# A state-space and expert block on one core: expert weights in pairs of units, more gathered rows per unit, six splits moved to GpSimd, two loads moved ahead

## The chip, the core and the metric

One core of a Trainium2 chip. The time is device microseconds from launch to end; it is the median of several runs, and lower is better. A profile is one execution recorded by the hardware profiler; its span runs from the first to the last instruction.

## What is computed

One layer on 512 frames of 1024 channels (with 16 meta frames ahead of them): a state-space mixer and a gated short convolution are merged into the stream `h`; then an expert layer (PEER) adds to it, and a last norm gives the output. The change touches only the expert layer:

```python
q = (xb @ w_q).reshape(PEER_BLOCK, PEER_HEADS, 2, PEER_HALF)
s = jnp.einsum('thjd,hjkd->thjk', q, sub_keys)      # 8 heads x 2 halves x 128 keys
sv, si = lax.top_k(s, 16)                           # then the best 16 of 16 x 16 sums
eidx = i1 * 128 + i2;  g = softmax(cs)              # 128 experts of 16384 per frame
act = gelu(einsum('td,thkd->thk', xb, u[eidx]))
out = einsum('thk,thkd->td', g * act, v[eidx])
```

All is float32; the large products are made from splits of each operand into a rounded part (hi) and a remainder (lo), with three matmuls for one.

## The kernel before, in words

The expert layer has 512 frames: 128 of them (tile 0) take their 128 + 128 expert rows by gather, the other 384 (`TD`) take all 16384 experts densely, in 128 units of 128 experts. Its work stands in four stretches.

1. **Routing** (lines 642 to 687). 16 query tiles; VectorE (DVE) picks the best 16 of every score tile (`top16`, lines 634 to 639, five instructions for each of 64 lists, more later in `choose`).
2. **The first 72 U units** (`S_AHEAD`, lines 902 to 917). For each unit `Stream` (lines 139 to 163) loads a 512 KB tile `raw` on SyncE's (SP's) queue, ScalarE (ACT) rounds it to `whi` (line 155), DVE makes `wlo` (line 156; an argument `lo` may name GpSimd, POOL, for chosen units), and TensorE (PE) does 24 matmuls of 384 columns into `sps`. Three `whi`/`wlo` buffers exist. ACT makes the gelu `so` (line 896), SP stores it to scratch `asc` (line 905). Beside that DVE makes the dense gates, which go to scratch `gsc` (lines 911 and 917).
3. **First V stretch**, n = 0 to 55 of the loop at lines 972 to 986. PE does the remaining 56 U units (three ahead, line 973) and for each n 18 matmuls of 512 columns of V (line 983) into `vps`. The weights of a unit (lines 957 to 966) are `wt` = gelu x gates (DVE, line 963), `wh` (ACT, line 964) and `wl` (DVE, line 965), each 128 x 384, made two units ahead (`WLEAD`); four `wh` and `wl` buffers. Gates come from `gsc` in tiles `gt` for four units (line 939). The V tile of a unit is loaded (line 152) and split (lines 155, 156) one unit ahead.
4. **Second V stretch**, n = 56 to 127: V alone, with the gelu reloaded from `asc` (line 946). The matmuls of the last three units are done together, frame tile by frame tile (`VTAIL`, line 977).

**The gathered rows** (lines 856 to 878) run beside stretches 3 and 4: POOL issues an indirect load of one row tile (line 862, four ahead, six buffers), DVE takes it (line 872 for 128 U rows, then line 874 for 128 V rows). How many are taken per unit is written out by hand: after unit n the program takes rows until 1.15 x `RATE` is used up, a row being 1.15 (`ROW`), with `RATE` 2.7 in stretch 3 and 1.0 in stretch 4. What is left stands behind the loop (line 987). Rows of unit n are queued on DVE behind that unit's V split and behind the last `wl` (line 985).

Then `final` (lines 575 to 602) goes through the four frame tiles: for tiles 1 to 3 the V sums are added (line 587), two squares with a sum on ACT (line 588), small DVE steps (lines 591 to 594, `rsqrt` at 127 to 132), two scalings (599, 601) and two stores (602). Tile 0 needs the last gathered row.

The order of the instructions on each engine is fixed when the program is built: a planner goes by program order, and lets a later instruction pass one that it expects to wait.

Of the kernel before, what the change touches and what calls it, by code (L numbers as in the profile page):

```python
# [11 lines left out]
F32 = mybir.dt.float32  # L12
R = mybir.dt.float32r
# [4 lines left out]
OP = mybir.AluOpType  # L18
# [4 lines left out]
P = 128  # L23
D = 1024
# [12 lines left out]
NK = 128  # L37
# [4 lines left out]
TD = T - P  # L42
# [6 lines left out]
S_FIRST = 5  # L49
HALVED = 3  # L50
PLAG = 2
S_BUFS = 4
ROW = 1.15
BUDGET = 3.1
GY = 0.2
# [1 line left out]
GT = 32  # L57
GL = 4
RLEAD = 4
WLEAD = 2  # L60
VTAIL = 3
RATE = (2.7, 1.0)


def build(nc, tc, ctx, a):
    def pool(name, bufs=1, space=None, stack=None, **kw):
        if space is not None:
            kw["space"] = space
        return (stack or ctx).enter_context(tc.tile_pool(name=name, bufs=bufs, **kw))

    V = nc.vector
    A = nc.scalar
    PL = nc.gpsimd
# [10 lines left out]
    rawp = pool("rawp", bufs=4)  # L84
    hlp = pool("hlp", bufs=3)
# [53 lines left out]
    class Stream:  # L139
# [6 lines left out]
            self.i, self.q, self.ahead = 0, [], ahead  # L146
            self.lo = lo or (lambda i: V)

        def _emit(self):
            i = self.i  # L150
            r = self.rawp.tile([P, D], F32, name="raw", tag="raw")
            self.load = nc.sync.dma_start(r, self.ap[self.order[i]])
            hi = self.hlp.tile([P, D], R, name="whi", tag="whi")
            lo = self.hlp.tile([P, D], R, name="wlo", tag="wlo")
            A.copy(hi, r)  # L155
            self.last = self.lo(i).tensor_tensor(lo, r, hi.bitcast(F32), op=OP.subtract)  # L156
            self.q.append((hi, lo))
            self.i += 1

        def next(self):  # L160
            while self.i < self.n and len(self.q) < 1 + self.ahead:
                self._emit()
            return self.q.pop(0)

    def norm_rows(pl, tiles, rows, ss):
# [30 lines left out]
    with xst:  # L196
# [46 lines left out]
        e = pi.tile([P, 5, H], F32, name="sp_e")  # L243
        z = pi.tile([P, 5, H], F32, name="sp_z")
        z2 = pi.tile([P, 5, H], F32, name="sp_z2")
        q = pi.tile([P, 5, H], F32, name="sp_q")
# [23 lines left out]
        act = pi.tile([H, NT, P], F32, name="act")  # L270
# [171 lines left out]
    def step():  # L442

        for q in scans[:2]:
            q[1] += 1
            if next(q[0], True):
                scans.remove(q)
            if scans and scans[0] is q and q[1] < 7:
                break
# [54 lines left out]
    for d in range(KD):  # L504
        ps_y = psC.tile([P, T], F32, name="ps_y", tag="ps_y")
        for u in range(2):
            hi, lo = wb.next()
# [5 lines left out]
        hi, lo = wb.next()  # L513
# [21 lines left out]
    with ExitStack() as st:  # L535
# [12 lines left out]
        for tp in range(2):  # L548
            pss = [[psC.tile([P, T], F32, name="ps_o", tag=("ps_y", "ps_c")[hf]) for hf in range(2)]
                   for _ in range(2)]  # L550
            for u in range(8):
                hi, lo = wo.next()
# [7 lines left out]
            for ti in range(2):  # L560
                t = 2 * tp + ti
                for hf in range(2):
                    o = slice(hf * 512, (hf + 1) * 512)
# [11 lines left out]
    def final(out, psp, lnf):  # L575
        with ExitStack() as st:
            pf = pool("pf", bufs=2, stack=st)
            nc.sync.dma_start(lnf, a["ln_final"].partition_broadcast(P))
            for t in range(NT):
# [15 lines left out]
                for hf in range(2):  # L595
# [6 lines left out]
                    nc.sync.dma_start(a["out"][t * P:(t + 1) * P, cs_], o)  # L602

    peer(nc, tc, ctx, a, pool, dram, rawp, hlp, ident, Stream, mm3, acc, u2h, u2l, u2d, ft512, psS, final)


def peer(nc, tc, ctx, a, pool, dram, rawp, hlp, ident, Stream, mm3, acc, u2h, u2l, u2d, ft512, psS, final):

    V, A, PL, PE = nc.vector, nc.scalar, nc.gpsimd, nc.tensor
    gsc = dram.tile([TD // GT, P, NK, GT], F32, name="gsc")  # L610
    asc = dram.tile([S_AHEAD, P, TD], F32, name="asc")
# [10 lines left out]
    sdot = pk.tile([P, PH * TOPK], F32, name="sdot")  # L622
    S_out = pool("sout", bufs=S_BUFS, stack=pp)

# [255 lines left out]
    def advance(gen, us):  # L880
        while us > 0:
            c = next(gen, None)
            if c is None:
                return us
            us -= c
        return us

    us = Stream(a["u_t"], rawp, hlp, ahead=2)

    def scores(dst):  # L890
        ps = psS.tile([P, T], F32, name="sps", tag="s")
        hi, lo = us.next()
        for k in range(KD):
            ks = slice(k * P, (k + 1) * P)
            mm = mm3(ps[:, :TD], hi[:, ks], lo[:, ks], u2h[:, k, P:], u2l[:, k, P:], k == 0, k == KD - 1)
        return mm, A.activation(dst, ps[:, :TD], AF.Gelu)  # L896
# [3 lines left out]
    gdebt = 0.0  # L900
    debt = 0.0
    for e in range(S_AHEAD):
        o = S_out.tile([P, TD], F32, name="so", tag="so")
        mm, act = scores(o)
        nc.sync.dma_start(asc[e], o)
        with ExitStack() as after:
            for i in (mm, act, anchor[0]):
                if i is not None:
                    after.enter_context(tc.issue_after(i.ins))
            for _ in range(min(NSTORE, len(stores))):  # L910
                nc.sync.dma_start(*stores.pop(0))
            if e >= S_FIRST:
                debt = advance(gates, BUDGET + debt)
    for _ in gates:
        pass
    while stores:
# [7 lines left out]
    pv = pool("pv", bufs=2, stack=rows, side="right")  # L924
# [4 lines left out]
    order = list(range(S_AHEAD, NK)) + list(range(S_AHEAD))  # L929
    vs = Stream(a["v"].rearrange("(u p) d -> u p d", p=P), rawv, hlv, order=order,  # L930
                lo=lambda i: V)
    out = [psV.tile([P, 2, 512], F32, name=f"vps{t}", tag=f"vps{t}") for t in range(ND)]
    loaded = {}

    def load_gates(n):
        if n % GL == 0:
            e = order[n]
            loaded["gt"] = pv.tile([P, TD // GT, GL, GT], F32, name="gt", tag="gt")
            nc.sync.dma_start(loaded["gt"], gsc[:, :, e:e + GL].rearrange("h p i t -> p h i t"))
        return loaded["gt"][:, :, n % GL]  # L940

    def load_gelu(n):
        if n % 2 == 0:
            e = order[n]
            loaded["al"] = rawp.tile([P, D], F32, name="raw", tag="raw")[:, :2 * TD].rearrange("p (i t) -> p i t", i=2)
            nc.sync.dma_start(loaded["al"], asc[e:e + 2].rearrange("i p t -> p i t"))
        return loaded["al"][:, n % 2]

    direct, wlast = [], [None]

    def ahead(n):
        if n < NK - S_AHEAD:
            o = S_out.tile([P, TD], F32, name="so", tag="so")
            scores(o)
            direct.append(o)

    def weights(n):
        gt = load_gates(n)
        ac = direct.pop(0) if order[n] >= S_AHEAD else load_gelu(n)
        wt = pv.tile([P, TD], F32, name="wt", tag="wt")  # L960
        wh = pv.tile([P, TD], R, name="wh", tag="wh", bufs=4)
        wl = pv.tile([P, TD], R, name="wl", tag="wl", bufs=4)
        V.tensor_tensor(wt.rearrange("p (h t) -> p h t", t=GT), ac.rearrange("p (h t) -> p h t", t=GT), gt, op=OP.mult)
        A.copy(wh, wt)  # L964
        wlast[0] = V.tensor_tensor(wl, wt, wh.bitcast(F32), op=OP.subtract)
        return wh, wl

    for n in range(S_BUFS - 1):
        ahead(n)
    q = [weights(n) for n in range(WLEAD)]  # L970
    tail = []
    for n in range(NK):
        ahead(n + S_BUFS - 1)
        if n + WLEAD < NK:
            q.append(weights(n + WLEAD))
        tail.append((n, *q.pop(0), *vs.next()))
        if n < NK - VTAIL or n == NK - 1:
            for t in range(ND):
                sl = slice(t * P, (t + 1) * P)
                for hf in range(2):  # L980
                    o = slice(hf * 512, (hf + 1) * 512)
                    for m, wh, wl, vh, vl in tail:
                        mm3(out[t][:, hf], wh[:, sl], wl[:, sl], vh[:, o], vl[:, o], m == 0, m == NK - 1)
            tail = []
        with tc.issue_after(vs.last.ins), tc.issue_after(wlast[0].ins):
            gdebt = advance(gen, ROW * RATE[order[n] < S_AHEAD] + gdebt)
    for _ in gen:
# [69 lines left out]
```

## Time and profile before

| | |
|---|---|
| median of 3 runs | 2101.83 us (2100.64 to 2103.62) |
| the profiled execution's own time | 2100.64 us |
| its span | 2098.9 us |
| TensorE matmul busy | 2005.3 us, 96% |
| VectorE, ScalarE, GpSimd busy | 71%, 44%, 24% |
| mean granted TensorE clock | 0.98 of full speed |

The profiled execution is the fastest of the three runs, 1.19 us under the median. Its own time is 1.74 us more than its span. A share of busy time is a mean over stretches; what a stretch is limited by is read inside it.

### The profile page before, as it was taken

To read this page: it belongs to the slowest core of one execution; us is meant where nothing else is said; L and a number is where in the kernel's file an instruction comes from. 1 tells how busy PE (TensorE), PEld (TensorE's weight loads), DVE (VectorE), ACT (ScalarE), POOL (GpSimd) and SP (SyncE) were. 2 spreads that over 40 slices of the span, in tenths; PEclk is the share of its full clock that TensorE was granted. 3 is DMA by queue.
4 is the path that set the end of the run, shared out by engine and by line. 5 is a ranking of instruction groups with operands and counts; after the bars stand their busy time and mean duration, and the time that the engine had idled before them with its cause. 6 is when DMAs were issued, how large, how long until landed. Compare 5 with 4: busy or idle time off the path is not lost.

```text
span 2098.9 us, 31321 instructions
## 1 busy us (share of the span) xinstructions
PE 2005.3 (96%) x11944; PEld 1826.4 (87%) x11944; DVE 1498.1 (71%) x2838; ACT 933.5 (44%) x1345; POOL 510.9 (24%) x434
## 2 busy tenths in 40 slices
PE   6999999999999998999999999999999999999990
PEld 6999999999888887889999998899999998888870
DVE  6677777754322254699679787887787779888887
ACT  4877777622222243333347586333333333333321
POOL 2222222200000002410000001565565544222234
PEclk9999999999999998999999999999999999999995
DMA  4323222222232353225547578999989989999967
GB/s 146 118 95 96 96 91 90 82 81 91 91 100 91 101 202 102 98 72 172 185 171 273 184 277 319 395 396 343 331 306 331 325 298 374 382 359 350 357 215 271
DMA packets 177574, 443.78 MB, mean 211 GB/s; under 512 B 14480, under 2 KB 82288, under 8 KB 177296
## 3 DMA queue, kind: packets, MB, share of 16 engines
q1 hardware_dynamic: 136816, 294.82, 40.9%
q0 software_dynamic: 40320, 145.40, 19.2%
q8 instruction: 93, 1.52, 0.3%
q10 hardware_dynamic: 288, 1.57, 0.2%
q14 instruction: 57, 0.47, 0.1%
HBM read 399.72 MB, written 42.01 MB: 210 GB/s over the span
## 4 chain that ended last, share of the span: by engine, by line
PE 80%; issue 10%; DVE 4%; POOL 3%; DMA 1%; ACT 1%; SPq 0%; POOLq 0%; ACTq 0%; DVEq 0%
PE pj L228 13%; PE sps L135 8%; PE sps L137 8%; PE sps L136 8%; PE vps L135 5%; PE vps L136 5%; PE vps L137 5%; POOL row L862 3%; PE f L136 2%; PE f L135 2%; PE f L137 2%; PE gps L802 2%; PE pz L136 1%; PE pz L137 1%; PE pz L135 1%
## 5 line engine op out<-in xcount | busy, mean ns | idle before, releaser
L155 ACT CAST whi<-raw 128x1024 fp32r<-128x1024 f32 x401 | 420.7, 1050 | 726.3 <-PE sps L136 266.5
L156 DVE TENSOR_TENSOR wlo<-raw,whi 128x1024 fp32r<-128x1024 f32 x383 | 470.8, 1231 | 318.7 <-ACT whi L155 305.9
L137 PE MATMUL sps<-u2h,wlo 128*128 128x384 f32 x1024 | 344.4, 336 | 3.4 <-DVE wlo L156 3.4
L135 PE MATMUL sps<-u2h,whi 128*128 128x384 f32 x1024 | 346.0, 338 | 1.0 <-ACT so L896 1.0
L136 PE MATMUL sps<-u2l,whi 128*128 128x384 f32 x1024 | 344.3, 336 | 0.0
L135 PE MATMUL vps<-whi,wh 128*128 128x512 f32 x768 | 298.9, 390 | 3.3 <-ACT whi L155 3.3
L136 PE MATMUL vps<-wlo,wh 128*128 128x512 f32 x768 | 299.2, 390 | 0.0
L137 PE MATMUL vps<-whi,wl 128*128 128x512 f32 x768 | 298.9, 389 | 0.0
L862 POOL DMA_INDIRECT row<-u,eix x128 | 209.4, 1636 | 172.2 <-DVE row L872 134.7
L862 POOL DMA_INDIRECT row<-v,eix x128 | 147.0, 1149 | 259.8 <-DVE acc L874 233.8
L137 PEld LDWEIGHTS sps<-u2h,wlo 128*128 128x128 f32 x1024 | 193.5, 189 | 3.8 <-DVE wlo L156 3.7
L135 PEld LDWEIGHTS sps<-u2h,whi 128*128 128x128 f32 x1024 | 193.6, 189 | 3.4 <-ACT so L896 1.3
L136 PEld LDWEIGHTS sps<-u2l,whi 128*128 128x128 f32 x1024 | 193.5, 189 | 2.0
L964 ACT CAST wh<-wt 128x384 fp32r<-128x384 f32 x128 | 65.8, 515 | 270.4 <-PE vps L136 166.7
L135 PEld LDWEIGHTS vps<-whi,wh 128*128 128x128 f32 x768 | 144.0, 188 | 31.8 <-ACT whi L155 3.8
L137 PEld LDWEIGHTS vps<-whi,wl 128*128 128x128 f32 x768 | 144.1, 188 | 30.2
L136 PEld LDWEIGHTS vps<-wlo,wh 128*128 128x128 f32 x768 | 144.2, 188 | 28.3 <-DVE wlo L156 0.3
L874 DVE SCALAR_TENSOR_TENSOR acc<-row,sdot,acc 128x1024 f32<-128x1024 f32 x128 | 163.9, 1280 | 6.0 <-DMA row<-v,eix 4.7
L228 PE MATMUL pj<-ul,whi 128*128 128x264 f32 (+1 forms) x784 | 161.6, 286 | 4.5 <-DVE ul L186 4.5
L228 PE MATMUL pj<-uh,whi 128*128 128x264 f32 (+1 forms) x784 | 164.9, 290 | 0.6 <-ACT uh L185 0.6
L228 PE MATMUL pj<-uh,wlo 128*128 128x264 f32 (+1 forms) x784 | 161.7, 286 | 0.0
L872 DVE SCALAR_TENSOR_TENSOR row<-row,u2t 128x1024 f32<-128x1024 f32 x128 | 150.1, 1220 | 0.0
(287 smaller groups left out, 3634.8 us busy)
## 6 DMA issues: line engine op xcount, KB each, us to landing
raw<-u_t SPq DMA_DIRECT2D x128, 512.0 KB
raw<-v SPq DMA_DIRECT2D x128, 512.0 KB
raw<-w_a SPq DMA_DIRECT2D x73, 512.0 KB
gsc<-gst SPq DMA_DIRECT2D x48, 512.0 KB
gt<-gsc SPq DMA_DIRECT2D x32, 768.0 KB
raw<-w_b SPq DMA_DIRECT2D x40, 512.0 KB
asc<-so SPq DMA_DIRECT2D x72, 192.0 KB
raw<-asc SPq DMA_DIRECT2D x36, 384.0 KB
```

What stands on the lines that cost most here:

```text
L135: PE.matmul(ps, lh, rh, start=start, stop=False)
L136: PE.matmul(ps, lh, rl, start=False, stop=False)
L137: return PE.matmul(ps, ll, rh, start=False, stop=stop)
L155: A.copy(hi, r)
L156: self.last = self.lo(i).tensor_tensor(lo, r, hi.bitcast(F32), op=OP.subtract)
L228: PE.matmul(ps[:, hf, :w], w_[:, ks], u_[:, k, off + hf * w:off + (hf + 1) * w], start=(k == 0 and q == 0), stop=(k == KD - 1 and q == 2))
L802: PE.matmul(ps[:, i], oi[:, j, 1], og[:, j, x], start=x == 0, stop=x == 1)
L862: PL.indirect_dma_start(out=row, out_offset=None, in_=a["uv"[i // n]], in_offset=bass.IndirectOffsetOnAxis(ap=eix[:, i % n:i % n + 1], axi ...
L872: V.scalar_tensor_tensor(row, row, 1.0, u2t, op0=OP.mult, op1=OP.mult, accum_out=sdot[:, k])
L874: V.scalar_tensor_tensor(acc[:, 0], row, sdot[:, k], acc[:, 0], op0=OP.mult, op1=OP.add)
L964: A.copy(wh, wt)
```

## The change

- `weights` makes `wt`, `wh` and `wl` for two units in one instruction each (128 x 768), every other n. The buffers of `wh` and `wl` go from four of one unit to two of two units; those of `wt` stay two, of twice the size. The gelu tiles `so` are made for two units too (two buffers of two units, where four of one were), and stored to `asc` in pairs, 36 stores of 384 KB where 72 of 192 KB were.
- The program takes 3.2 gathered rows per unit in stretch 3 (was 2.7), 1.1 in stretch 4 (was 1.0).
- The remainder `wlo` of the first six U units is made on GpSimd.
- The first two V tiles are loaded and split ahead of the first weights, so ahead of the first load of gates.

```diff
-S_BUFS = 4
+S_BUFS = 2
+S_POOL = 6
-WLEAD = 2
-RATE = (2.7, 1.0)
+RATE = (3.2, 1.1)
...
-    us = Stream(a["u_t"], rawp, hlp, ahead=2)
+    us = Stream(a["u_t"], rawp, hlp, ahead=2, lo=lambda i: PL if i < S_POOL else V)
...
     for e in range(S_AHEAD):
-        o = S_out.tile([P, TD], F32, name="so", tag="so")
-        mm, act = scores(o)
-        nc.sync.dma_start(asc[e], o)
+        if e % 2 == 0:
+            o = S_out.tile([P, 2, TD], F32, name="so", tag="so")
+        mm, act = scores(o[:, e % 2])
+        if e % 2:
+            nc.sync.dma_start(asc[e - 1:e + 1].rearrange("i p t -> p i t"), o)
...
     def weights(n):
         gt = load_gates(n)
         ac = direct.pop(0) if order[n] >= S_AHEAD else load_gelu(n)
-        wt = pv.tile([P, TD], F32, name="wt", tag="wt")
-        wh = pv.tile([P, TD], R, name="wh", tag="wh", bufs=4)
-        wl = pv.tile([P, TD], R, name="wl", tag="wl", bufs=4)
+        wt = pv.tile([P, 2, TD], F32, name="wt", tag="wt")
+        wh = pv.tile([P, 2, TD], R, name="wh", tag="wh")
+        wl = pv.tile([P, 2, TD], R, name="wl", tag="wl")
...
-        return wh, wl
-
-    for n in range(S_BUFS - 1):
+        q.extend((wh[:, i], wl[:, i]) for i in range(2))
+
+    for n in range(3):
         ahead(n)
-    q = [weights(n) for n in range(WLEAD)]
-    tail = []
+    for _ in range(2):
+        vs.emit()
+    q, tail = [], []
+    weights(0)
     for n in range(NK):
-        ahead(n + S_BUFS - 1)
-        if n + WLEAD < NK:
-            q.append(weights(n + WLEAD))
+        ahead(n + 3)
+        if n % 2 and n + 1 < NK:
+            weights(n + 1)
```

## Rows read from the trace of the kernel before

**Rows 1.** The page's first lines: the span, then busy time, share of the span and instructions of TensorE and VectorE among the engines.

```profile
span 2098.9 us, 31321 instructions
PE 2005.3 (96%) x11944; PEld 1826.4 (87%) x11944; DVE 1498.1 (71%) x2838; ACT 933.5 (44%) x1345; POOL 510.9 (24%) x434
```

**Rows 2.** The last stretch of 50 us: length, then busy us (instructions) of PE, weight loads, DVE, ACT, POOL, the granted clock, the share of the DMA engines and GB/s.

```profile
2050.00:2100.00 50.00, 0.00 (x0) 0.00 (x0) 38.43 (x83) 7.90 (x20) 19.96 (x18) 0.50 0.70 263
```

**Rows 3.** Who waited for whom, TensorE, whole span: total us, times, longest.

```profile
PE sps L137 <- DVE wlo L156: 3.4, 1, 3.4
PE vps L135 <- ACT whi L155: 3.3, 1, 3.3
...
PE sps L135 <- ACT so L896: 1.0, 1, 1.0
```

**Rows 4.** Stretches, the DVE instructions of line 874 (V rows) alone: length, DVE busy (count), granted clock, DMA share, GB/s. The first also holds all 128 U rows of line 872.

```profile
1306.00:1748.00 442.00, 29.92 (x24) 1.00 0.96 342
1748.00:2031.00 283.00, 90.36 (x71) 1.00 0.97 344
2031.00:2084.00 53.00, 43.61 (x34) 0.63 0.83 296
```

**Rows 5.** The last matmul in the timeline of PE (start, us, what).

```profile
2041.21 0.39 PE L137 MATMUL vps<-whi,wl 128*128 128x512 f32 x1
```

**Rows 6.** The end in the timeline of DVE: the last add of V sums, the last rows, a small step of the last norm and the last scaling.

```profile
2044.22 0.68 DVE L587 TENSOR_TENSOR acc<-acc,vps 128x512 f32<-128x512 f32 x1
...
2081.08 2.72 DVE L874 SCALAR_TENSOR_TENSOR acc<-row,sdot,acc 128x1024 f32<-128x1024 f32 x2 [1.64 <-DMA row<-v,eix]
...
2094.23 0.16 DVE L132 SCALAR_TENSOR_TENSOR r<-rsq_t,r 128x1 f32<-128x1 f32 x1
2094.42 0.75 DVE L601 SCALAR_TENSOR_TENSOR acc<-acc,r,row 128x512 f32<-128x512 f32 x1
```

**Rows 7.** The first square of `final` in the timeline of ACT.

```profile
2083.83 0.60 ACT L588 ACTIVATE junk<-acc 128x512 f32<-128x512 f32 x1 [53.58 <-DVE acc L874]
2084.36 0.19 ACT L588 ACTIVATION_READ_ACCUMULATOR junk<-acc 128x1 f32 x1
```

**Rows 8.** DVE where the fourth U unit waits.

```profile
942.18 0.28 DVE L637 MATCH_REPLACE8 tmp<-sv,ssb 128x128 f32<-128x128 f32 x1
942.37 1.22 DVE L156 TENSOR_TENSOR wlo<-raw,whi 128x1024 fp32r<-128x1024 f32 x1
```

**Rows 9.** PE behind that wait, at half clock and at full clock.

```profile
943.65 0.69 PE L137 MATMUL sps<-u2h,wlo 128*128 128x384 f32 x1 [3.39 <-DVE wlo L156]
...
947.98 0.52 PE L135 MATMUL sps<-u2h,whi 128*128 128x384 f32 x1
948.30 0.47 PE L136 MATMUL sps<-u2l,whi 128*128 128x384 f32 x1
...
949.30 0.33 PE L135 MATMUL sps<-u2h,whi 128*128 128x384 f32 x1
949.47 0.33 PE L136 MATMUL sps<-u2l,whi 128*128 128x384 f32 x1
```

**Rows 10.** Groups by line, engine and operation, whole span: count, busy us, mean ns of one, idle time ahead of them and its releasers.

```profile
L156 DVE TENSOR_TENSOR wlo<-raw,whi 128x1024 fp32r<-128x1024 f32 x383 | 470.8, 1231 | 318.7 <-ACT whi L155 305.9 <-PE gps L802 10.7
L155 ACT CAST whi<-raw 128x1024 fp32r<-128x1024 f32 x401 | 420.7, 1050 | 726.3 <-PE sps L136 266.5 <-issue 110.0 <-PE f L136 97.3
...
L874 DVE SCALAR_TENSOR_TENSOR acc<-row,sdot,acc 128x1024 f32<-128x1024 f32 x128 | 163.9, 1280 | 6.0 <-DMA row<-v,eix 4.7
...
L965 DVE TENSOR_TENSOR wl<-wt,wh 128x384 fp32r<-128x384 f32 x128 | 71.3, 558 | 71.5 <-ACT wh L964 71.2
...
L156 POOL TENSOR_TENSOR wlo<-raw,whi 128x1024 fp32r<-128x1024 f32 x18 | 43.4, 2411 | 104.5 <-ACT whi L155 104.5
```

**Rows 11.** SP's queue where V begins.

```profile
1288.78 2.84 SPq L917 DMA_DIRECT2D gsc<-gst  x4
...
1296.05 0.38 SPq L939 DMA_DIRECT2D gt<-gsc  x1
1297.16 1.93 SPq L152 DMA_DIRECT2D raw<-v  x3
```

**Rows 12.** ACT at the same place.

```profile
1303.57 0.98 ACT L964 CAST wh<-wt 128x384 fp32r<-128x384 f32 x2 [5.28 <-DVE wt L963]
1304.45 1.99 ACT L155 CAST whi<-raw 128x1024 fp32r<-128x1024 f32 x2
```

**Rows 13.** PE at the same place.

```profile
1306.50 1.26 PE L135 MATMUL vps<-whi,wh 128*128 128x512 f32 x3 [3.26 <-ACT whi L155]
```

**Rows 14.** Stretches, columns as in rows 2: inside stretch 3, where the two meet, inside stretch 4.

```profile
1350.00:1690.00 340.00, 340.00 (x1733) 310.78 (x1732) 272.27 (x397) 124.32 (x168) 190.27 (x114) 1.00 0.95 340
...
1739.30:1763.80 24.50, 24.50 (x110) 20.27 (x108) 24.47 (x29) 9.09 (x12) 16.72 (x10) 1.00 1.04 386
...
1764.00:2028.00 264.00, 264.00 (x1166) 218.60 (x1165) 222.57 (x259) 95.11 (x130) 62.23 (x65) 1.00 0.97 345
```

**Rows 15.** What DVE waited for inside stretch 4 (1764 to 2028 us): total, times, longest.

```profile
DVE wl L965 <- ACT wh L964: 38.3, 64, 0.7
DVE wlo L156 <- ACT whi L155: 0.8, 2, 0.4
```

**Rows 16.** A stretch of 5 us early in stretch 3, columns as in rows 2.

```profile
1380.00:1385.00 5.00, 5.00 (x30) 4.84 (x29) 4.42 (x8) 1.89 (x3) 2.95 (x3) 1.00 1.03 410
```

More of the change, by code (lines that the diff above doesn't have):

```diff
@@ L147, in __init__, with emit @@
             self.lo = lo or (lambda i: V)
-        def _emit(self):
+        def emit(self):
             i = self.i
@@ L161, in next @@
             while self.i < self.n and len(self.q) < 1 + self.ahead:
-                self._emit()
+                self.emit()
             return self.q.pop(0)
@@ L939, in load_gates @@
             nc.sync.dma_start(loaded["gt"], gsc[:, :, e:e + GL].rearrange("h p i t -> p h i t"))
-        return loaded["gt"][:, :, n % GL]
+        return loaded["gt"][:, :, n % GL:n % GL + 2]
     def load_gelu(n):
[L943 to L947, printed above, removed]
+        e = order[n]
+        al = rawp.tile([P, D], F32, name="raw", tag="raw")[:, :2 * TD].rearrange("p (i t) -> p i t", i=2)
+        nc.sync.dma_start(al, asc[e:e + 2].rearrange("i p t -> p i t"))
+        return al
     direct, wlast = [], [None]
@@ L952, in ahead @@
         if n < NK - S_AHEAD:
-            o = S_out.tile([P, TD], F32, name="so", tag="so")
-            scores(o)
-            direct.append(o)
+            if n % 2 == 0:
+                direct.append(S_out.tile([P, 2, TD], F32, name="so", tag="so"))
+            scores(direct[-1][:, n % 2])
     def weights(n):
@@ L959, in weights @@
         ac = direct.pop(0) if order[n] >= S_AHEAD else load_gelu(n)
-        wt = pv.tile([P, TD], F32, name="wt", tag="wt")
-        wh = pv.tile([P, TD], R, name="wh", tag="wh", bufs=4)
-        wl = pv.tile([P, TD], R, name="wl", tag="wl", bufs=4)
-        V.tensor_tensor(wt.rearrange("p (h t) -> p h t", t=GT), ac.rearrange("p (h t) -> p h t", t=GT), gt, op=OP.mult)
+        wt = pv.tile([P, 2, TD], F32, name="wt", tag="wt")
+        wh = pv.tile([P, 2, TD], R, name="wh", tag="wh")
+        wl = pv.tile([P, 2, TD], R, name="wl", tag="wl")
+        V.tensor_tensor(wt.rearrange("p i (h t) -> p i h t", t=GT), ac.rearrange("p i (h t) -> p i h t", t=GT),
+                        gt.rearrange("p h i t -> p i h t"), op=OP.mult)
         A.copy(wh, wt)
         wlast[0] = V.tensor_tensor(wl, wt, wh.bitcast(F32), op=OP.subtract)
-        return wh, wl
-    for n in range(S_BUFS - 1):
+        q.extend((wh[:, i], wl[:, i]) for i in range(2))
+    for n in range(3):
         ahead(n)
-    q = [weights(n) for n in range(WLEAD)]
-    tail = []
+    for _ in range(2):
+        vs.emit()
+    q, tail = [], []
+    weights(0)
     for n in range(NK):
-        ahead(n + S_BUFS - 1)
-        if n + WLEAD < NK:
-            q.append(weights(n + WLEAD))
+        ahead(n + 3)
+        if n % 2 and n + 1 < NK:
+            weights(n + 1)
         tail.append((n, *q.pop(0), *vs.next()))
```

## The prediction

> **What bounds the kernel now.** I read the page's shares first, then the waits, then the end. TensorE is busy for 2005.3 of 2098.9 us, VectorE for 71% [rows 1], so the total is TensorE's chain of matmuls plus whatever stands ahead of, between and behind them. The waits of TensorE are few; three matter here: 3.4 us for a remainder `wlo`, 1.0 us for `so` right ahead of it, and 3.3 us for a `whi` of V [rows 3]. The largest idle piece is in no wait, because TensorE has nothing more to do: in the last 50 us it does nothing at all [rows 2]. Its last matmul ends at 2041.21 + 0.39 = 2041.6 us [rows 5], so 57.3 us stand behind it. In them VectorE works off gathered rows: 24 V rows (and all 128 U rows) are done by 1748 us, 71 more by 2031 us, and 34 remain [rows 4]. The last row ends at 2081.08 + 2.72 = 2083.8 us [rows 6]; only then ScalarE, 53.58 us idle, starts the squares of `final` [rows 7], which takes the last 15.1 us.
>
> **The rows per unit.** 56 x 2.7 + 72 x 1.0 = 223 of 256 rows are taken inside the loop now, which fits the 34 counted (one crosses a border). After the change 56 x 3.2 = 179.2, and 1.1 x 69 = 75.9 brings the sum to 255.1: the last row is taken at n = 124, with the V matmuls of three units still ahead of TensorE. So behind the last matmul stands only what needs the last V sum: one add 0.68 [rows 6], one square 0.60 + 0.19 [rows 7], 12 small steps at a pitch of 0.19 = 2.3, one scaling 0.75, and the stores from 2095.17 to 2098.9 = 3.7 [rows 6]; with handovers 8.5 us. The other end is 15.1 us, if all of `final` still stands there. I take 9, as the parts are rows of the same steps: 57.3 - 9 = 48.3 us saved (42.2 to 48.8).
>
> What pays for the earlier rows is VectorE's free time. In stretch 4 it is busy 222.57 of 264 us [rows 14]; 1166 matmuls are 64.8 units of 4.08 us, so 3.43 us a unit. Pairs take two instructions out per pair: by the 1231 ns for 1024 columns and the 558 ns for 384 [rows 10], 1.05 ns a column, one of 768 takes 0.96 us where two take 1.12, so 0.31 us less per pair; 0.2 rows of 1.28 us add 0.26. That gives 6.82 of 8.16 us a pair. In stretch 3, 272.27 us over 1733/42 = 41.3 units is 6.6 a unit [rows 14], 13.2 a pair; one row more and 0.31 less make 14.2 of 16.5. Both fit, so I cost them at nothing, under TensorE's matmuls. The cover is thinnest where the stretches meet: there the rate of stretch 3 meets the short units, and VectorE is full, 24.47 of 24.50 us, with TensorE not yet waiting [rows 14]. Three units at half a row more are 1.9 us of added work there. I take 0, and 2 us for the high end.
>
> A pair also shortens the lead: `wh` of a pair must wait until the pair before last has left its buffer, and must be ready two units later (8.16 us in stretch 4) instead of three (12.2). Behind that wait on ScalarE stand V casts, behind `wl` on VectorE the rows. Chain: a cast of at most 0.98 (two single ones [rows 12]), `wl` 0.96, then a V cast, split and rows: some 5 us. Nothing lost.
>
> GpSimd has to issue 0.5 rows more per unit of stretch 3 and is busy 190 of 340 us there [rows 14]; covered. Pairs of `so` halve the stores on SP's queue, each of which waits for a gelu with the next U load behind it; the even ones no longer do that. A buffer of `so` is stored one unit later than now, with three units of 4.16 us left: nothing.
>
> **Six U splits on GpSimd.** The fourth U unit waits on TensorE because its `wlo` stands in VectorE's queue behind the top-16 lists and starts at 942.37 us [rows 8]. The idle time is 3.39 + 1.0 (the interleaved fifth unit's wait [rows 3]), and then the granted clock is at its lower level, 1.2 GHz: matmuls 0.32 us apart up to 948.30, then 0.17 [rows 9], 15 of them, 2.2 us. Together 6.6. On GpSimd one split takes 2.41 us [rows 10], with the cast of 1.05 us 3.5 us, beside 8.3 us of matmuls of the two other buffered units; GpSimd has no row to issue there. All six leave VectorE's queue, so the seventh unit's split, on VectorE again, finds it shorter. Ends: 0 (the wait goes to the seventh) and 6.6; I take 6.
>
> The row that speaks against it is the price itself, 2411 against 1231 ns. The Trainium skill ("SBUF — State Buffer", on the shared port pair) says that a VectorE instruction with two SBUF inputs and a GpSimd one that reads SBUF lock each other out for a whole instruction. By it VectorE would stand up to 6 x 2.41 = 14.5 us, and the sum would lose these 6 us. No row here has the two side by side, and the lists take one tensor.
>
> **First V loads ahead of the gates.** Now `gt` goes first at 1296.05, behind the last gate stores, and V follows at 1297.16 [rows 11]. ScalarE waits 5.28 us for the first `wt`, then casts weights, then V [rows 12]; TensorE starts V at 1306.50 after 3.26 us [rows 13]. With V first, its casts fill ScalarE's wait. But `gt` starts 1.1 us later, behind 1 MB, 2.6 us at 410 GB/s [rows 16], and the paired steps are 0.8 us longer. Ends: all of it is saved, with 1.7 us at the lower clock (5.0 us); or weights ready at 1304.1 + 4.5 = 1308.6, 2 us worse. U matmuls of the next unit can fill the gap, since their operands are there; I take 2.5 saved.
>
> **The sum.** Span 2098.9 - 48.3 - 6 - 2.5 = 2042.1. The profiled execution's own time is 1.74 us over its span and 1.19 under the median: **2045.0 us**. With all good ends 2098.9 - 48.8 - 6.6 - 5.0 + 2.9 = 2041.4; with all bad ones 2098.9 - 42.2 + 2 + 2 + 2.9 = 2063.6.
>
> **Rivals.**
>
> *Transfers become the bound.* From 1306 to 2084 us 342 x 442 + 344 x 283 + 296 x 53 = 264.2 MB move [rows 4]. To be done when TensorE ends at 2033, from 1297.5 on, they need 359 GB/s, and stretch 4 shows 345 at a share of 0.97 [rows 14]. If 344 were what this mix can have, they end at 2065.5, and 15.1 + 2.9 behind that gives **2084**. Against it: 386 GB/s where the stretches meet [rows 14], 410 early [rows 16], and VectorE never waits for a row inside the loop: the 4.7 us for rows [rows 10] lie in the end. Chance 0.09.
>
> The Trainium skill ("DMA: Bandwidth & Descriptors", "Where 436 GB/s comes from") puts a core's part of HBM at about 358 GB/s. By it the transfers would end at 2035.5 and the run at 2054; the trace disagrees, with 386 and 410.
>
> *The rows still do not get done.* If VectorE gets behind, and half of the 34 rows stay behind the loop: 34 rows take 2031 to 2083.8, 1.55 us each; 17 take 26.4, 10.6 of them beside the last matmuls: 2033 + 15.8 + 15.1 + 2.9 = **2067**. For it: the full VectorE at the meeting of the stretches. Against: 1.3 us free per pair behind it. Chance 0.05.
>
> *VectorE becomes the bound, slower.* In stretch 4 it waits 0.6 us a unit for `wh` [rows 15] and not for V casts, because weights come singly and fill that time. If in pairs the longer cast (0.98) and both V casts (2 x 1.05 [rows 10]) stand open, a pair takes 6.82 + 3.1 = 9.9 us: 1.75 over TensorE's 8.16, times 36 is 63 us, **2108**. It decides once open waits pass 1.34 us a pair. Against: a waits-only loss shrinks as VectorE falls behind, since the casts are then done. Chance 0.07.
>
> **How the numbers follow.** A measurement of this kernel can tell 0.2%, 4 us. The forecast has 0.77, transfers 0.09, rows left 0.05, VectorE 0.07; 0.02 for gains and losses that cancel. Faster 0.77 + 0.09 + 0.05 = 0.91, same 0.02, slower 0.07. The range takes the forecast's ends with some us at the low one for idle bits that I left out: 2038 to 2066.
>
> **What would show it.** Right: no row of line 874 after the last matmul; last matmul near 2033, span end 8 to 10 us behind it; no wait of a U unit near 940; a wait under 2 us at the first V matmul; clock 1.00 at both places. Wrong: rows behind the loop; TensorE waits for `wl`, `wlo` or `whi` once per pair; VectorE waits for rows from DMA inside the loop; `gt` landing later than V and TensorE idle longer there.

## The result

The changed kernel takes **2051.76 us** (median of 4 runs, 2049.34 to 2052.51) against 2101.23 us for the kernel before: a ratio of 0.9761, 95% interval 0.9744 to 0.9778. The forecast was 2045.0 us, in a range of 2038 to 2066; it came out 6.8 us, 0.3%, too low. The profiled execution took 2052.23 us.

### The profile page after: what moved, and what is told of

It reads as the page before. It is cut to its first block, busy times and chain, and to the rows that moved or that the text cites. A ratio compares the mean times of both kernels' runs of the same rounds, so it can differ in the third digit from the quotient of the medians.

```text
span 2050.5 us, 31037 instructions
## 1 busy us (share of the span) xinstructions
PE 2006.5 (98%) x11944; PEld 1825.3 (89%) x11944; DVE 1476.2 (72%) x2704; ACT 925.0 (45%) x1281; POOL 551.3 (27%) x440
## 4 chain that ended last, share of the span: by engine, by line
PE 89%; DVE 6%; DMA 2%; ACT 1%; SPq 1%; issue 1%; POOL 0%; ACTq 0%; POOLq 0%
PE pj L228 13%; PE vps L135 8%; PE vps L136 8%; PE vps L137 8%; PE sps L135 7%; PE sps L136 7%; PE sps L137 7%; PE f L136 2%; PE f L135 2%; PE f L137 2%; PE gps L802 2%; PE pz L136 1%; PE qps L135 1%; PE pz L137 1%; PE pz L135 1%; PE qps L136 1%
## 5 line engine op out<-in xcount | busy, mean ns | idle before, releaser
L156 DVE TENSOR_TENSOR wlo<-raw,whi 128x1024 fp32r<-128x1024 f32 x377 | 461.5, 1230 | 310.3 <-ACT whi L155 297.4
L862 POOL DMA_INDIRECT row<-v,eix x128 | 176.1, 1375 | 218.4 <-DVE acc L874 191.9
L967 ACT CAST wh<-wt 128x768 fp32r<-128x768 f32 x64 | 53.6, 838 | 178.6 <-PE vps L136 100.9
```

What stands on the lines that cost most here:

```text
L862: PL.indirect_dma_start(out=row, out_offset=None, in_=a["uv"[i // n]], in_offset=bass.IndirectOffsetOnAxis(ap=eix[:, i % n:i % n + 1], axi ...
```

## The profile after

The page's first lines; rows 1 answer to them.

```profile
span 2050.5 us, 31037 instructions
PE 2006.5 (98%) x11944; PEld 1825.3 (89%) x11944; DVE 1476.2 (72%) x2704; ACT 925.0 (45%) x1281; POOL 551.3 (27%) x440
```

TensorE does the same work in a span 48.4 us shorter. Where that lies is seen at the end. The last matmul in PE's timeline, and stretches with the DVE instructions of line 874 alone (length, DVE busy with their count, granted clock, DMA share, GB/s), which answer to [rows 4, 5]:

```profile
2039.78 0.39 PE L137 MATMUL vps<-whi,wl 128*128 128x512 f32 x1
```

```profile
1748.00:1860.00 112.00, 43.75 (x35) 1.00 1.06 385
1860.00:2031.00 171.00, 57.26 (x45) 1.00 0.90 325
2031.00:2051.00 20.00, 0.00 (x0) 0.81 0.27 105
```

No V row is taken after 2031 us, where 34 were left before. Behind the last matmul (2039.78 + 0.39 = 2040.17) stand 10.3 us, where 57.3 stood. In DVE's timeline that is the last add of V sums and the last scaling:

```profile
2041.35 0.68 DVE L587 TENSOR_TENSOR acc<-acc,vps 128x512 f32<-128x512 f32 x1
...
2045.87 0.75 DVE L601 SCALAR_TENSOR_TENSOR acc<-acc,r,row 128x512 f32<-128x512 f32 x1
```

So 47.0 us came from the end, and the last matmul itself moved only from 2041.6 to 2040.2, although two waits on the way were to go. TensorE's waits, whole span (total us, times, longest), answer to [rows 3]:

```profile
PE sps L135 <- ACT so L896: 2.7, 1, 2.7
PE vps L135 <- ACT whi L155: 1.9, 1, 1.9
...
PE vps L137 <- DVE wl L968: 0.3, 1, 0.3
```

The 3.4 us for `wlo` near 940 are gone. The wait at the first V matmul is 1.9 us (was 3.3). But the 2.7 us for `so` are new: they are not the 1.0 us of before, which stood near 940. Two places in stretches (length, then busy us and instructions of PE, weight loads, DVE, ACT, POOL, the granted clock, DMA share, GB/s): around the fourth U unit, and where V begins.

```profile
900.00:950.00 50.00, 50.00 (x282) 46.52 (x282) 44.41 (x287) 19.13 (x27) 16.90 (x8) 1.00 0.32 104
...
1296.00:1312.00 16.00, 14.08 (x60) 12.00 (x59) 13.79 (x18) 6.78 (x8) 11.49 (x8) 0.89 1.03 401
1312.00:1340.00 28.00, 25.03 (x117) 21.92 (x117) 19.37 (x27) 8.92 (x11) 12.36 (x10) 0.94 1.05 390
```

At 940 TensorE is busy throughout at 2.4 GHz. From 1312 to 1340 it loses 3 us of idle time, and the mean clock of 0.94 says that 3.4 of 28 us ran at 1.2 GHz. The DMA engines are full from 1296 on (a share of 1.03 to 1.05). In the kernel before they were as full from 1312 on, and TensorE was busy throughout:

```profile
1312.00:1340.00 28.00, 28.00 (x138) 24.79 (x137) 20.66 (x33) 9.12 (x12) 14.58 (x11) 1.00 1.05 391
```

SP's queue and ACT where V begins; [rows 11, 12] answer to them.

```profile
1290.79 0.37 SPq L941 DMA_DIRECT2D gt<-gsc  x1
1291.97 1.88 SPq L152 DMA_DIRECT2D raw<-v  x4
1293.89 0.43 SPq L152 DMA_DIRECT2D raw<-u_t  x1
1294.36 0.43 SPq L941 DMA_DIRECT2D gt<-gsc  x1
1294.84 12.99 SPq L152 DMA_DIRECT2D raw<-v  x1
```

```profile
1297.08 0.83 ACT L967 CAST wh<-wt 128x768 fp32r<-128x768 f32 x1 [4.34 <-DVE wt L965]
...
1324.34 1.99 ACT L155 CAST whi<-raw 128x1024 fp32r<-128x1024 f32 x2 [17.67 <-DMA raw<-v]
1326.24 0.48 ACT L896 ACTIVATE so<-sps 128x384 f32<-128x384 f32 x1
```

Two things are to be seen. The gates still go first: "V ahead of the gates" did not happen on the queue. And the fifth V load is issued for 13 us and lands at 1324.3; ScalarE stands before its cast for 17.67 us, and the gelu `so` that TensorE needs stands behind that cast on the same engine. TensorE goes on at once when `so` is there:

```profile
1326.77 0.69 PE L135 MATMUL sps<-u2h,whi 128*128 128x384 f32 x1 [2.68 <-ACT so L896]
```

In the kernel before, the same gelu (the 78th) came at almost the same time, and behind a late V cast too:

```profile
1324.73 1.05 ACT L155 CAST whi<-raw 128x1024 fp32r<-128x1024 f32 x1 [4.04 <-DMA raw<-v]
1325.68 0.48 ACT L896 ACTIVATE so<-sps 128x384 f32<-128x384 f32 x1
```

There TensorE did not wait for it. It began V at 1306.50 [rows 13], and begins now at 1298.91, 7.6 us earlier. The V loads are issued 5.2 us earlier too (1291.97, before 1297.16 [rows 11]), but this gelu comes no sooner. So part of what was gained ahead of V is lost again where the tiles land no earlier than they did.

## The experiments

Theory: the rates give nearly all, the GpSimd splits some 6 us, the pairs and the early V loads nothing, and the lost microseconds lie where V begins, because the DMA is full there. Rivals: the pairs make the room for the rows; the loss is one of order on ScalarE.

**e1: the kernel before with the new rates alone.**

```diff
-RATE = (2.7, 1.0)
+RATE = (3.2, 1.1)
```

> The kernel before with only the new rates 3.2 and 1.1; single weights, all splits on VectorE. Theory (the rows give the gain alone, and TensorE covers them): the last row is taken before the last matmul, the 57.3 us behind it become about 10, so 2101.2 - 47 = 2054; the wait for wlo near 940 stays (3.4 us) and so does the one ahead of the first V matmul. If the rows of the first units also make the new wait for so near 1325 (2.7 us and the lower clock behind it, 4.5 together), that wait is here too and the time is 2059. Rival (the pairs make the room for the rows): VectorE, without the 0.31 us a pair saved, falls behind in the second V stretch; TensorE waits for wl or wlo there again and again, and the time is over 2065.

2054.99 us, ratio 0.978 (0.9765 to 0.9795): 45.5 of the 49.5 us. TensorE's waits:

```profile
PE vps L136 <- DVE wlo L156: 3.7, 2, 3.4
PE sps L137 <- DVE wlo L156: 3.4, 1, 3.4
```

The second line is the old wait near 940. The first is new, at 1331.5 us, 7 us later than that of the changed kernel and behind another tile. With such a wait the expectation had 2059; it came out 4 us better. VectorE keeps up without pairs. The rows bring the gain, and they alone, in the kernel before, bring a new wait with them.

**e2: the changed kernel with the old rates** (the diff of e1 turned round).

> The changed kernel with the old rates 2.7 and 1.0. Theory: 34 rows stand behind the loop again and some 57 us behind the last matmul, so 2051.8 + 47 = 2099, less up to 4.5. Theory A (rows of the first units fill the DMA queues, the fifth V tile lands late, and the gelu so stands behind its cast on ScalarE): with 2.7 rows a unit the wait for so near 1325 falls under 1 us, and the time is 2094 to 2096. Rival B (the order of casts on ScalarE, which the change altered, makes it whatever the rows): the wait stays 2 to 3 us, and the time is 2098 to 2100.

2096.9 us, 0.9981 (0.9972 to 0.999); 57.6 us stand behind the last matmul (2037.0) again. The wait for `so` is 2.1 us, where theory A wanted under 1: rival B by the wait, neither by the time. ACT:

```profile
1322.13 1.99 ACT L155 CAST whi<-raw 128x1024 fp32r<-128x1024 f32 x2 [17.12 <-DMA raw<-v]
```

The fifth V tile lands 2.2 us earlier, no more. So the rate alone does not make the wait; in three units 2.7 and 3.2 differ by one or two rows, and four more are sent ahead in both kernels, so that this was a weak test of what the rows do.

**e3: all U splits on VectorE.**

```diff
-S_POOL = 6
+S_POOL = 0
```

> The changed kernel with all U splits on VectorE again. Theory: the fourth U unit waits near 940 for wlo (3.4 us) and its neighbour for so (1.0), with some 2 us at the lower clock: 2051.8 + 6.6 = 2058.4. Rival (the six splits on GpSimd cost VectorE what they saved, or the wait came back elsewhere): under 2 us of difference.

2058.8 us, 0.9797 (0.9783 to 0.981), and the 3.4 us for `wlo` and 1.0 for `so` are back near 940. The interval lies just above the changed kernel's (to 0.9778) and overlaps that of e7, which runs the same queues (to 0.9785); what carries the verdict is the profile. The wait for `so` where V begins is longer here, 4.8 us, so that not all of the 7 us belong to the splits.

**e4: single weights and single `so`**, the rest as changed.

```diff
-        wt = pv.tile([P, 2, TD], F32, name="wt", tag="wt")
-        wh = pv.tile([P, 2, TD], R, name="wh", tag="wh")
+        wt = pv.tile([P, TD], F32, name="wt", tag="wt")
+        wh = pv.tile([P, TD], R, name="wh", tag="wh", bufs=4)
...
-    weights(0)
+    q = [weights(n) for n in range(WLEAD)]
```

> The changed kernel with the weights made one unit at a time, two ahead, and so stored one unit at a time, as before; rates, GpSimd splits and the early V loads stay. Theory (pairs are worth nothing, since VectorE has room in both stretches): 2051.8 within 3 us. If the wait for so near 1325 is made by the pairs (a pair of weights and its casts come at once), it goes, and the time is near 2047; if by the rows, it stays. Rival (the pairs pay for the rows): TensorE waits for wl in the second V stretch and the time is over 2060.

2048.86 us (2046.77 to 2049.99), 0.9753 (0.9739 to 0.9766). The wait for `so` is gone; a 2.5 us wait at the first V matmul and 0.6 for a `wlo` stay. The pairs bring nothing; the median is 3 us better without them, at the edge of what the intervals can tell. By its expectation, a wait for `so` that goes here is made by the pairs. The rows are the same as in the changed kernel, and the gelu that stands at 1326.24 there stands at 1320.46 here, so the order that the pairs give has a part in the wait, beside the rows.

**e5: no rows in the first three units.**

```diff
-            gdebt = advance(gen, ROW * RATE[order[n] < S_AHEAD] + gdebt)
+            gdebt = advance(gen, ROW * (0.0 if n < 3 else 3.4 if n < 56 else 1.1) + gdebt)
```

> The changed kernel, with no gathered row in the first three units of the first V stretch and 3.4 a unit in the rest of it. With 2.7 rows a unit the wait for so near 1323 was still 2.1 us, so that the rate alone does not make it. Theory (the rows of the four transfers ahead and of the first units share the DMA, which is full from 1293 on, half and half with the tiles of V and U, so that the fifth V tile lands at 1324): without them it lands before 1315, the wait for so is under 0.5 us, the clock stays at 1.00 behind it, and the time is 2051.8 - 4.5 = 2047. Rival (the order on ScalarE: the gelu stands behind two casts of V, whenever the rows come): the wait stays over 2 us, the time within 2 us of 2052.

2047.7 us (2045.84 to 2048.11), 0.9751 (0.9738 to 0.9764), and the last matmul ends at 2034.0. ACT and the stretch from 1296 to 1340, first of this kernel:

```profile
1314.67 2.00 ACT L155 CAST whi<-raw 128x1024 fp32r<-128x1024 f32 x2 [9.01 <-DMA raw<-v]
```

```profile
1296.00:1340.00 44.00, 42.06 (x210) 37.45 (x208) 31.57 (x39) 18.36 (x23) 21.23 (x14) 1.00 1.05 392
```

and the same stretch of the changed kernel:

```profile
1296.00:1340.00 44.00, 39.11 (x176) 33.92 (x175) 33.16 (x44) 15.70 (x19) 23.85 (x17) 0.92 1.04 394
```

The V tile lands 10 us earlier and TensorE has no wait for `so`, while the order of casts and gelu on ScalarE is as before. The DMA engines move the same 392 to 394 GB/s in both; what changed is whose bytes they are. In the changed kernel the two queues share the engines from 1288 to 1335 us nearly half and half; in e5 SP's queue has three quarters (packets, MB, share of 16 engines; q1 carries the tiles and gates of SP, q0 the rows; the changed kernel first, then e5):

```profile
q1 hardware_dynamic: 5873, 9.41, 55.7%
q0 software_dynamic: 2304, 8.39, 45.6%
```

```profile
q1 hardware_dynamic: 7517, 12.78, 76.1%
q0 software_dynamic: 1325, 4.84, 26.5%
```

That settles it against the rival of order alone: the order lets a late tile stop the gelu, and the gathered rows make the tile late. It does not make the rows the only cause: e4 takes the same wait away with all its rows. Either edit is enough, and how the loss divides between rows and pairs stays open.

**e6: V truly ahead of the gates.**

```diff
-            nc.sync.dma_start(loaded["gt"], gsc[:, :, e:e + GL].rearrange("h p i t -> p h i t"))
+            with tc.issue_after(vs.load.ins):
+                nc.sync.dma_start(loaded["gt"], gsc[:, :, e:e + GL].rearrange("h p i t -> p h i t"))
```

> The changed kernel, with the first load of gates held until the first two V loads are issued, so that SyncE's queue has V, V, gates, V, V, gates (the change as it stands leaves the gates first). Theory: the gates land some 2.6 us later (1 MB ahead of them at 390 to 410 GB/s) and are what TensorE's first V matmul waits for: its wait grows from 1.9 to 3 to 4.5 us, and the time is 2053 to 2055. Rival (the V casts then stand ahead of the weights on ScalarE and fill its idle 4.3 us, so that the wait goes): under 1 us, and 2049 to 2050.

2054.37 us, 0.9784 (0.977 to 0.9798): as the theory had it in the total, but with a far longer wait at the first V matmul than its 3 to 4.5 us. TensorE's wait and ACT there:

```profile
PE vps L135 <- ACT wh L968: 9.3, 1, 9.3
```

```profile
1308.07 0.83 ACT L968 CAST wh<-wt 128x768 fp32r<-128x768 f32 x1 [7.51 <-DVE wt L966]
```

The gates are issued at 1293.19 behind two V loads, with two more behind them. VectorE's `wt` starts at 1307.08, 11.1 us later than in the changed kernel (1296.02), where the expectation had 2.6. TensorE idles 9.3 us at once, and then has no wait near 1325, by when the V tiles had that time to land. So this order moves the loss. Whether it makes it larger is not clear: the median is 2.2 us over that of e7, and their runs overlap.

**e7: without the early V loads.**

```diff
-    for _ in range(2):
-        vs.emit()
```

> The changed kernel without the two lines that emit V tiles ahead of the first weights. The planner builds the same instructions in the same order on all five engines' queues. Theory: the same time as the changed kernel, 2051.8 within 2 us, the first V matmul after a wait of 1.9 us and the wait for so near 1325 of 2.7. There is no rival but the spread of the measurement, which this run gives on another chip.

2052.16 us (2050.13 to 2053.09), 0.9771 (0.9758 to 0.9785): the same time. But its waits are not the same ones, with the same instructions in the same order:

```profile
PE vps L135 <- ACT whi L155: 3.4, 1, 3.4
...
PE vps L135 <- ACT wh L967: 1.4, 1, 1.4
```

3.4 + 1.4 + 0.3 = 5.1 us here and 1.9 + 2.7 + 0.3 = 4.9 us in the changed kernel. A wait for a transfer in a full stretch is not fixed to one tile; in these two profiles the sum is the same. Changes of 1 to 2 us in one of these waits, between two profiles, say nothing.

**e8: 60 splits on GpSimd.**

```diff
-S_POOL = 6
+S_POOL = 60
```

> The changed kernel with the splits of the first 60 U units on GpSimd in place of 6, so that they run beside VectorE's gate work, whose one-hot instructions read two SBUF tensors (oi 1219 ns, og 685 ns, eq 1220 ns). Theory (GpSimd's splits and VectorE do not hold each other up): oi, og and eq keep their means within 3%, the GpSimd split stays at 2.39 us, and the time is 2052 within 4 us. Rival (they lock each other out): where a split falls beside them the means of oi, og or eq rise by 10% and more, up to 54 x 2.4 = 130 us in all, VectorE (272 of 336 us busy from 960 to 1296) becomes late with the gates, and the time rises by over 10 us.

2059.45 and 2075.12 us in two runs, 0.9844 (0.981 to 0.9879); the profile is of the first. Groups of DVE from 925 to 1296 us (count, busy us, mean ns, idle time before), first the changed kernel, then this one:

```profile
L820 DVE TENSOR_TENSOR og<-oi,cG 128x1024 f16<-128x1024 f16 x96 | 61.0, 685 | 0.2
L739 DVE TENSOR_TENSOR eq<-eq,sf 128x2048 f16<-128x2048 f16 x8 | 9.8, 1221 | 0.1
L636 DVE FIND_INDEX8 ci<-cv,cd 128x8 uint32<-128x112 f32 x32 | 8.7, 271 | 0.0
...
L730 DVE CAST wf<-wb 128x128 f16<-128x128 f32 x4 | 1.1, 266 | 0.0
```

```profile
L820 DVE TENSOR_TENSOR og<-oi,cG 128x1024 f16<-128x1024 f16 x96 | 87.2, 954 | 0.2
L739 DVE TENSOR_TENSOR eq<-eq,sf 128x2048 f16<-128x2048 f16 x8 | 16.0, 2002 | 0.1
L636 DVE FIND_INDEX8 ci<-cv,cd 128x8 uint32<-128x112 f32 x32 | 8.6, 269 | 0.0
...
L730 DVE CAST wf<-wb 128x128 f16<-128x128 f32 x4 | 7.7, 1915 | 0.0
```

The expected theory fell. Instructions with two SBUF tensors are stretched: two `og` in a row take 3.38 us beside a split and 1.29 without one, in DVE's timeline of this kernel:

```profile
1119.92 3.38 DVE L820 TENSOR_TENSOR og<-oi,cG 128x1024 f16<-128x1024 f16 x2
...
1129.00 1.29 DVE L820 TENSOR_TENSOR og<-oi,cG 128x1024 f16<-128x1024 f16 x2
```

The split that stands beside the first took 3.03 us, in place of 2.39: either engine may be the one that waits. The lists (line 636) are untouched. But a cast of one tensor (line 730) is stretched too, from a mean of 0.27 to 1.92 us, so that the number of tensors read is not all that counts. The late one-hot work then reaches TensorE (4.1 us for `og` at 1131, and the lower clock behind it). The Trainium skill's rule on the shared port pair ("SBUF — State Buffer", "Who interferes with whom") says just this of a VectorE instruction with two SBUF inputs beside a GpSimd one that reads SBUF, and the run agrees.

**e9: U units four ahead of V, not three.**

```diff
-    for n in range(3):
+    for n in range(4):
...
-        ahead(n + 3)
+        ahead(n + 4)
```

> The changed kernel with the U units made four ahead of V in place of three (the two pairs of so hold four units, so that no memory is added); rates as changed. Theory (from 1293 to 1340 the transfers are the limit, and TensorE waits for whatever lands late): one more U unit, 4.2 us of matmuls, stands ahead of the first V matmul, so that the wait there (1.9 us, and 1.7 for the lower clock) goes, and V is wanted 4.2 us later at each unit, which takes the wait of 2.7 us too: the last matmul near 2033, the time 2044 to 2046. Rival (the gelu of the fifth unit then waits for a buffer of so, and stands on ScalarE ahead of the V casts): TensorE waits 2 us and more for whi or so, 2050 and over.

2048.02 us (2047.69 to 2048.97), 0.9752 (0.9739 to 0.9766). Half of the theory held: no wait near 1325. The other half did not: the first V matmul still waits, 2.9 us for `whi` at 1297.9, since the planner put the first V matmuls ahead of the added unit.

**e10: e9 and e5 together.**

> The two edits together: U units four ahead, and no gathered row in the first three units, 3.4 a unit after them in the first V stretch. Theory: both waits near 1297 and 1325 are under 0.5 us and the clock stays at 1.00 from 825 to the end: 2047.7 less 1.9 and 1.7 gives 2044. Rival (rows so late that the last of them stand behind the last matmul, or TensorE waits for so): 2047 and over.

2047.31 us (2046.65 to 2047.35), 0.9748 (0.9735 to 0.9761), not 2044: the wait near 1325 is gone, the one at the first V matmul stays (2.2 us). The two edits cure the same wait and do not add.

**e11: e4 and e5 together.**

> The changed kernel with single weights and single so, and no gathered row in the first three units. Theory (the pairs bring nothing, and single weights and late rows both take the wait near 1325, each alone, so that they do not add): 2047 to 2049, the same as either alone. Rival (the pairs cost 3 us by themselves, in another place): 2044 to 2045.

2045.68 us (2044.59 to 2046.74), 0.9741 (0.9728 to 0.9754): between what theory and rival gave, and the fastest of all. It beats the kernel before by 2.6% and lies some 6 us below both runs of the changed program (2051.76 and 2052.16), with no overlap of their runs. TensorE's waits from V on:

```profile
PE vps L136 <- ACT whi L156: 1.9, 1, 1.9
...
PE vps L137 <- DVE wlo L157: 0.3, 1, 0.3
```

**e12: the rows shifted into the second V stretch.**

```diff
-RATE = (3.2, 1.1)
+RATE = (2.7, 1.5)
```

> The changed kernel with rates 2.7 and 1.5: the same rows inside the loop (the last at n = 126), but taken from the first V stretch to the second, where VectorE is then busy 6.82 + 2 x 0.4 x 1.28 = 7.84 of 8.16 us a pair by the estimate, 0.32 us of room. Theory (VectorE keeps up as long as its work fits): no wait of TensorE in the second V stretch, the last rows near the end of the loop, 2049 to 2053. Rival (waits for casts that stand open on VectorE add 0.4 us and more a pair, and VectorE is the limit): TensorE waits for wl or wlo once per pair, or the last ten rows and more stand behind the last matmul, and the time is over 2058.

2067.16 us, 0.9853 (0.9835 to 0.9871): the rival's time, but not its cause. ACT's longest wait, 1740 to 2030 us, then two stretches (columns as above):

```profile
ACT whi L155 <- DMA raw<-v: 131.7, 42, 6.1
```

```profile
1850.00:1900.00 50.00, 48.36 (x206) 37.91 (x206) 45.58 (x42) 15.96 (x17) 26.44 (x18) 1.00 1.06 385
1900.00:1950.00 50.00, 47.24 (x201) 36.94 (x200) 41.58 (x39) 15.21 (x16) 22.75 (x17) 1.00 1.06 386
```

and the same of the changed kernel, where ACT had no wait for a transfer:

```profile
1850.00:1900.00 50.00, 50.00 (x222) 41.38 (x222) 42.18 (x39) 17.02 (x18) 16.80 (x13) 1.00 1.06 384
1900.00:1950.00 50.00, 50.00 (x222) 41.40 (x221) 42.77 (x39) 17.28 (x19) 19.82 (x15) 1.00 1.05 378
```

VectorE is not full in these 100 us (45.6 and 41.6 of 50 us), and where it is, from 1740 to 1800 (59.48 of 60 us), TensorE is busy for all 60. The V tiles are late, and the DMA moves no more than in the changed kernel, 385 GB/s: it was already full at 1.1 rows a unit. This is the prediction's rival of transfers, one step further on.

## Why the prediction was right, and where it was not

**The rows: right.** No row behind the loop, 47.0 us from the end against 48.3. The end is 10.3 us, not 9. e1 shows that the rates alone do it. VectorE's estimate of 6.82 of 8.16 us a pair, 84%, came out as 42.2 to 42.8 of 50 us; `wt` and `wl` of a pair measured 0.95 and 0.96 us against 0.96. TensorE never waited there, nor where the stretches meet: 690.97 of 691 us from 1340 to 2031 are busy.

**The six splits: right.** 4.4 us of idle time and the lower clock went, 6 taken, 6.6 read from the trace, and e3 brings the same waits back. The lists beside them were not slowed, as the prediction had it. Its reason, that they take one tensor, is not shown to be the whole: e8 shows the weighed rule where two are read, but a cast of one tensor was stretched there as well.

**V ahead of the gates: wrong.** The step assumed that program order is queue order. The planner moved the gates first again, and without the two lines it builds the same queues (e7). Done in earnest (e6), V first makes TensorE wait 9.3 us. The wait at the first V matmul is 1.3 us shorter than before, not 2.5; that is not this step's doing, and in e7, with the same queues, it was 3.4 us again.

**"I cost them at nothing": the step that failed.** It priced the rows by VectorE and GpSimd, and the transfers by means over stretches 3 and 4, where 345 and 340 GB/s left room. The first 45 us of stretch 3 were not priced. There four rows ahead, three loads of gates, the first V tiles and U tiles all come at once on full engines. The price is 2.7 + 0.3 us of waits and 1.5 to 1.7 us of the lower clock. Of the 7.1 us by which the last matmul came later than the forecast's 2033.1, these are some 4.5. The V start did not give 1.2 us; the rows are not shown to cause that, since with the first of them held back (e5) it still waits 1.9 us. 1.2 us more is a later start of the query matmuls (821.4 against 820.3), which the change doesn't touch. The splits gave back 0.6, and 0.8 is left unassigned. In e5 the last matmul ends at 2034.0, close to the forecast, though in the fastest of its five runs; by medians it gains 4.1 us on the changed kernel.

The same step failed for the pairs: "Nothing lost" was worked out from leads inside stretch 4, not for the start of V, where e4, with single weights, has no wait for `so`. And the forecast of the total was helped by luck: the span came out 8.4 us over its 2042.1, while the 2.9 us from span to median came out as 1.3.

**Of the rivals**, the transfers were the right one, at a chance of 0.09, with the wrong ceiling: not 344 GB/s, since full stretches of these runs moved 378 to 394. From 1850 on the changed kernel stands at that ceiling (384 at a share of 1.06) without TensorE waiting; e12 steps over it. One sign of being wrong that the prediction named did show: VectorE waited for gathered rows inside the loop, 8.8 us in 10 times, all before 1500 us, without making TensorE wait. And the granted clock where V begins was 0.89 (1296 to 1312), where the forecast wanted 1.00. VectorE as the bound did not show in any run.

The 49.5 us gained is 47.0 us at the end and 1.4 us ahead of it in the profiled executions; the rest is the spread of runs.

## What to carry to other kernels

Read a shared resource in the 50 us where its users start together, not in the mean of the stretch: TensorE's new wait stood behind transfers that all began at once, and three units without rows took it away, as did weights made one unit at a time. An engine that is made to arrive earlier can find a wait that was hidden. Where an engine works in order, look at what stands behind the instruction that waits for a transfer; here a gelu behind a V cast. And before an edit of program order is priced, ask whether the planner keeps that order.

## What the hardware showed unexpectedly

- Where the DMA was full, the issue of one 512 KB load took 8 to 17 us (12.99 in the rows above, 8.16 in e1, 16.52 in e9), and the next load on SP's queue was issued only behind it.
- One core moved 378 to 394 GB/s for tens of microseconds, at a share of 1.04 to 1.06. The Trainium skill ("HBM Reference", "Specifications (TRN2)") says that a core that streams alone goes well above the 358 GB/s of its share, and these rows, of a program on one core, agree.
- A wait of 1.9 us ahead of the first V matmul was followed by 3.4 us at 1.2 GHz in the changed kernel, and by none in e5 and e11, where the wait was as long. The cost of a short wait is not fixed.
- Beside a GpSimd split, two VectorE products of 128x1024 f16 took 3.38 us in place of 1.29, and a 128x128 cast a mean of 1.92 in place of 0.27, while the top-16 instructions kept 269 to 271 ns.
